# Rotary key behind the first query tile, and cross-attention values by pairs of heads, in a two-layer decoder block on one core

## The chip, the core and the metric

The kernel runs on one core of a Trainium2 chip. A core has TensorE (PE in the profile; PEld is its weight load), VectorE (DVE), ScalarE (ACT), GpSimd (POOL) and SyncE (SP), each with a queue of its own that it works through in order; DMA is issued from SyncE's queue and, in the front, from ScalarE's. The metric is device time in microseconds; less is better.

## What is computed

A block of two decoder layers over 512 tokens of width 1024, all in float32. Layer 0 mixes tokens with multi-head latent attention (MLA), layer 1 with sparse attention (DSA); each layer then attends across into 256 memory tokens with four heads of width 256, and applies a SwiGLU network (FFN). Every sub-layer ends in a residual and a layer norm. Cut to what the change touches:

```python
def mla_mixer(x, pos, w_in, q_norm, w_uq, kv_norm, w_ukv, w_o):
    h = x @ w_in                                   # 512 query, 256 key/value, 32 rotary columns
    c_q, c_kv, k_rope = h[..., :512], h[..., 512:768], h[..., 768:]
    q = (rms_norm(c_q, q_norm) @ w_uq).reshape(b, s, 16, 96)
    q = jnp.concatenate([q[..., :64], apply_rope(q[..., 64:], pos)], axis=-1)
    kv = (rms_norm(c_kv, kv_norm) @ w_ukv).reshape(b, s, 16, 128)
    k_rope = apply_rope(k_rope[:, :, None, :], pos)   # one rotary key for all heads
    ...

# cross-attention of a layer, four heads:
q = x @ w_q; k, v = mem @ w_kv[:, :1024], mem @ w_kv[:, 1024:]
out = softmax(q k^T / 16) v @ w_o
```

## The kernel before

**Products.** Every float32 operand is split into a high part (a cast on ScalarE, `split` L99) and a low part (a subtraction on VectorE, L101). `mm3` (L122 to L124) makes one product of three matmuls: high by high, high by low, low by high. `chunk` (L112) loads 512 KB of weights on SyncE's queue into a buffer `raw`, of which there are three, and splits it into `wh` and `wl`, of which there are five each. In the profile a matmul stands as out<-moving, stationary; its columns are those of the moving operand.

**Order.** The Tile framework issues the program's operations in an order of its own that follows the code's order and the operands' dependences, and sets the waits; a buffer that comes round again waits for its last reader. PSUM has two pools of four banks, "a" and "b".

**Front.** `x` transposed (four 512 KB loads, the first in two parts, SyncE) and the key/value weights `w_ckv` (304 columns, four parts c of two k each: three on ScalarE's queue, the last on SyncE, L491) are split part by part, and 8 x 12 matmuls of 304 columns make `ps2`, the 256 key/value and 48 rotary columns of four token tiles. Then the rotary key is turned: ScalarE copies each tile's rotary columns (L521, 8 copies), TensorE transposes them (L522, 4), ScalarE copies the bank to `pk` (L524). The four query tiles follow (24 matmuls of 512 columns each, weights `w_cq` in four chunks); behind each, `rms_t` normalises the key/value tile and the query tile before it: the squares on ScalarE (L530), the root on GpSimd and VectorE (L277, L279), the product on VectorE (L533), transposes on TensorE (L536), a split. Between these VectorE computes the rotary angles (`trig`, L451 to L475). The query tiles end at 51.72 us, where the value product of the heads (`mla_v`) begins.

**Cross-attention.** One stage in each layer, 251.7 to 370 us and 1011.2 to 1129.7 us. For each head hd: `scores(hd)` (24 matmuls of 256 columns and the exponentials, L426), `q_proj(hd+1)` (48 of 512), `xa_kv(hd+1)`: keys (48 of 256), values (48 of 256, weights in two chunks of the head), and `pv(hd)`: it normalises the softmax weights, turns them (8 transposes, L766), splits them, and makes 12 matmuls of 512 columns. Out-projection and residual follow.

## Time and profile before

| | us |
|---|---|
| median of 3 runs | 1540.42 (1538.08 to 1541.06) |
| profiled execution | 1538.13 |
| its span, first to last instruction | 1536.3 |
| TensorE busy | 1503.6 (98%) |
| VectorE, ScalarE, GpSimd busy | 994.9, 650.2, 303.9 |

The page gives for each engine the busy time and its share of the span; a chain of waits followed back from the last instruction; and groups of like instructions. The granted clock of TensorE is shown as a share of full speed (2.4 GHz; its other level is 1.2 GHz), 0.996 over this span. Matmuls overlap by some 0.16 us, so the pace of a run is read from start to start, not from the length of one.

### The profile page before, as it was taken

To read this page: it belongs to the slowest core of one execution; us is meant where nothing else is said; L and a number is where in the kernel's file an instruction comes from. 1 tells how busy PE (TensorE), PEld (TensorE's weight loads), DVE (VectorE), ACT (ScalarE), POOL (GpSimd) and SP (SyncE) were. 2 spreads that over 40 slices of the span, in tenths; PEclk is the share of its full clock that TensorE was granted. 3 is DMA by queue.
4 is the path that set the end of the run, shared out by engine and by line. 5 is a ranking of instruction groups with operands and counts; after the bars stand their busy time and mean duration, and the time that the engine had idled before them with its cause. 6 is when DMAs were issued, how large, how long until landed. Compare 5 with 4: busy or idle time off the path is not lost.

```text
span 1536.3 us, 20733 instructions
## 1 busy us (share of the span) xinstructions
PE 1503.6 (98%) x7902; PEld 1283.5 (84%) x7902; DVE 994.9 (65%) x1741; ACT 650.2 (42%) x1158; POOL 303.9 (20%) x299
## 2 busy tenths in 40 slices
PE   8999999999999999999999989999999999999997
PEld 7788889988898888888888787898988888888886
DVE  7787868454746665654668988675448465656545
ACT  5677753343233333332246577344332433333230
POOL 1222001000032331400024653000002322324002
PEclk9999999999999999999999999999999999999999
DMA  6233424323333232233242147333323233222221
GB/s 214 71 98 107 155 83 134 125 85 97 124 97 101 77 124 97 96 97 108 84 138 87 51 158 240 110 119 102 110 94 125 83 110 98 102 94 90 97 96 55
DMA packets 51417, 166.45 MB, mean 108 GB/s; under 512 B 5300, under 2 KB 11972, under 8 KB 49268
## 3 DMA queue, kind: packets, MB, share of 16 engines
q1 hardware_dynamic: 50740, 164.18, 32.6%
q8 instruction: 62, 1.02, 0.3%
q10 hardware_dynamic: 576, 0.93, 0.2%
q14 instruction: 39, 0.32, 0.1%
HBM read 160.86 MB, written 9.47 MB: 111 GB/s over the span
## 4 chain that ended last, share of the span: by engine, by line
PE 88%; DVE 5%; ACT 3%; DMA 2%; issue 1%; POOL 1%; SPq 0%; POOLq 0%; DVEq 0%; ACTq 0%
PE ps L122 27%; PE ps L123 27%; PE ps L124 27%; DVE t L101 2%; PE ps L336 1%; ACT wh L99 1%; ACT t L426 1%; ACT t L99 1%; DMA raw<-in_w_cq_dram 1%; PE ps L1043 1%; PE ps L644 1%; DMA t<-in_xT_dram 1%; PE ps L1060 0%; POOL wl L101 0%; DMA t<-scr 0%
## 5 line engine op out<-in xcount | busy, mean ns | idle before, releaser
L122 PE MATMUL ps<-t,wh 128*128 128x512 f32 (+1 forms) x1256 | 456.2, 364 | 3.5 <-DVE t L101 3.4
L123 PE MATMUL ps<-t,wh 128*128 128x512 f32 (+1 forms) x1256 | 455.2, 362 | 0.8 <-DVE t L101 0.8
L124 PE MATMUL ps<-t,wl 128*128 128x512 f32 (+1 forms) x1256 | 454.9, 362 | 0.0
L99 ACT CAST wh<-raw 128x1024 fp32r<-128x1024 f32 (+3 forms) x219 | 227.4, 1038 | 450.0 <-PE ps L123 167.1
L101 DVE TENSOR_TENSOR wl<-raw,wh 128x1024 fp32r<-128x1024 f32 (+2 forms) x198 | 253.2, 1280 | 218.0 <-ACT wh L99 216.3
L122 PE MATMUL ps<-wh,t 128*128 128x512 f32 (+3 forms) x838 | 305.4, 364 | 1.1 <-ACT t L426 0.9
L123 PE MATMUL ps<-wl,t 128*128 128x512 f32 (+3 forms) x838 | 303.1, 362 | 1.2 <-DVE wl L101 1.2
L124 PE MATMUL ps<-wh,t 128*128 128x512 f32 (+3 forms) x838 | 303.0, 362 | 0.2 <-DVE t L101 0.2
L122 PEld LDWEIGHTS ps<-t,wh 128*128 128x128 f32 x1256 | 237.1, 189 | 41.5 <-DVE t L101 5.5
L123 PEld LDWEIGHTS ps<-t,wh 128*128 128x128 f32 x1256 | 237.2, 189 | 37.0 <-DVE t L101 1.3
L124 PEld LDWEIGHTS ps<-t,wl 128*128 128x128 f32 x1256 | 237.1, 189 | 36.6
L122 PEld LDWEIGHTS ps<-wh,t 128*128 128x128 f32 x838 | 158.5, 189 | 25.1 <-ACT t L426 1.3
L123 PEld LDWEIGHTS ps<-wl,t 128*128 128x128 f32 x838 | 158.4, 189 | 24.6 <-DVE wl L101 1.4
L124 PEld LDWEIGHTS ps<-wh,t 128*128 128x128 f32 x838 | 158.4, 189 | 24.0 <-DVE t L101 0.4
L99 ACT CAST t<-ps 128x512 fp32r<-128x512 f32 (+2 forms) x249 | 122.9, 525 | 129.3 <-PE ps L336 86.1
L279 POOL TENSOR_TENSOR sm<-sm,mhalf 128x1 f32<-128x1 f32 x32 | 28.6, 893 | 689.0 <-DVE sm L277 689.0
L101 DVE TENSOR_TENSOR t<-ps,t 128x512 fp32r<-128x512 f32 (+2 forms) x249 | 144.1, 607 | 20.3 <-ACT t L99 19.5
L99 ACT CAST wh<-t 128x1024 fp32r<-128x1024 f32 x56 | 58.9, 1052 | 141.9 <-PE ps L123 123.6
L101 DVE TENSOR_TENSOR wl<-t,wh 128x1024 fp32r<-128x1024 f32 x56 | 71.2, 1272 | 65.2 <-ACT wh L99 63.4
L863 DVE TENSOR_TENSOR t<-ps,t 128x512 f32<-128x512 f32 x44 | 30.4, 692 | 120.1 <-PE ps L124 120.1
L101 DVE TENSOR_TENSOR t<-t,t 128x512 fp32r<-128x512 f32 (+2 forms) x113 | 84.5, 751 | 23.0 <-ACT t L99 20.7
L99 ACT CAST t<-t 128x512 fp32r<-128x512 f32 (+2 forms) x113 | 64.5, 574 | 56.2 <-POOL t L797 33.6
(178 smaller groups left out, 1654.5 us busy)
## 6 DMA issues: line engine op xcount, KB each, us to landing
raw<-in_ffn_in_dram SPq DMA_DIRECT2D x88, 512.0 KB, 3.5
...
```

The source lines that it names most:

```text
L99: nc.scalar.copy(h, src)
L101: (eng or nc.vector).tensor_tensor(l, src, h.bitcast(F32), op=ALU.subtract)
L122: nc.tensor.matmul(ps, st[0], mv[0], start=start, stop=False, skip_group_check=more)
L123: nc.tensor.matmul(ps, st[0], mv[1], start=False, stop=False, skip_group_check=more)
L124: nc.tensor.matmul(ps, st[1], mv[0], start=False, stop=stop, skip_group_check=more)
L279: nc.gpsimd.tensor_tensor(b, a, mhalf, op=ALU.pow)
L336: nc.tensor.transpose(pt[:, k], x_of(tt)[:, 512 * n + P * k:512 * n + P * k + P], ident)
L426: nc.scalar.activation(Sx, src, AF.Exp, bias=nb, scale=scale, accum_out=self.sm[:, i:i + 1])
L644: nc.tensor.transpose(pt[:, P * qt:P * qt + P], Ss[qt][:, P * kb:P * kb + P], ident)
L863: nc.vector.tensor_tensor(sg, pu, sg, op=ALU.mult)
L1043: nc.tensor.transpose(pt[:, P * i:P * i + P], Ss[i][:, P * kb:P * kb + P], ident)
```

## The change

**Front.** `w_ckv` is laid out with all eight k side by side and is loaded into three buffers (k 0 to 2, of which k 0 alone first; 3 to 5; 6 and 7), all from ScalarE's queue and at once; its high and low parts lie in three buffers each. So the `w_cq` chunks come one `raw` buffer earlier in the ring. The loads of positions and constants are issued ahead of them. The rotary key is put into a function, `rope_key`, which is called behind the normalisation of the first key/value tile, that is behind the first query tile's matmuls.

**Cross-attention.** The value weights are laid out by pairs of heads. An even head makes the values of itself and of the next one: four chunks, and 48 matmuls of 512 columns into two banks, k outermost; an odd head makes none. Normalising, turning and splitting the softmax weights is a function of its own, `turned`, and is called ahead of `xa_kv(hd+1)`.

```diff
         return res
 
     raw_x = [t8(F32) for _ in range(2)]
-    def pairs_of(tile_):
-        return tile_[:, 0:2 * NC0].rearrange("p (k m) -> p k m", k=2)
-
-    raw_w = [pairs_of(wp.tile([P, 1024], F32, tag="raw", name=nm("raw"), bufs=3)) for _ in range(3)]
+    def threes(tag, dt, bufs=5):
+        ts = [wp.tile([P, 1024], dt, tag=tag, name=nm(tag), bufs=bufs) for _ in range(3)]
+        return [t[:, 0:3 * NC0].rearrange("p (k m) -> p k m", k=3) for t in ts]
+
+    raw_w = threes("raw", F32, 3)
     xr = A["xT"].rearrange("c p (k t) -> c p k t", k=2)
-    wr = A["w_ckv"].rearrange("c p (k m) -> c p k m", k=2)
-    for i in range(2):
+    wr = A["w_ckv"].rearrange("p (k m) -> p k m", k=NK)
+    for i, ks in enumerate((slice(0, 1), slice(1, 3))):
         nc.sync.dma_start(raw_x[0][:, i], xr[0, :, i])
-        nc.scalar.dma_start(raw_w[0][:, i], wr[0, :, i])
+        nc.scalar.dma_start(raw_w[0][:, ks], wr[:, ks])
     nc.sync.dma_start(raw_x[0][:, 2:4], xr[1])
-    nc.scalar.dma_start(raw_w[1], wr[1])
-    nc.scalar.dma_start(raw_w[2], wr[2])
+    nc.scalar.dma_start(raw_w[1], wr[:, 3:6])
     nc.sync.dma_start(raw_x[1][:, 0:2], xr[2])
+    nc.scalar.dma_start(raw_w[2][:, 0:2], wr[:, 6:8])
     nc.sync.dma_start(raw_x[1][:, 2:4], xr[3])
+    posi = t2(I32)
+    nc.sync.dma_start(posi, A["positions"].broadcast_to((P, S)))
+    nc.sync.dma_start(cst, A["consts"])
     NR, NC = 73, 7
 
     def general_bias():
...
     nc.gpsimd.memset(T0[0:64], 1.0)
     nc.gpsimd.memset(T1[64:128], 1.0)
     ps2 = [bank("b") for _ in range(NT)]
+    whs, wls = threes("wh", FR), threes("wl", FR)
+    w_parts = {0: (0, 0, 1), 1: (0, 1, 3), 2: (1, 0, 3), 6: (2, 0, 2)}
     for c in range(4):
         h, l = XT[c // 2]
-        if c == 3:
-            raw_w.append(pairs_of(wp.tile([P, 1024], F32, tag="raw", name=nm("raw"), bufs=3)))
-            nc.sync.dma_start(raw_w[3], wr[3])
-        rx, rw = raw_x[c // 2], raw_w[c]
-        wh = pairs_of(wp.tile([P, 1024], FR, tag="wh", name=nm("wh")))
-        wl = pairs_of(wp.tile([P, 1024], FR, tag="wl", name=nm("wl")))
+        rx = raw_x[c // 2]
         step = 1 if c == 0 else 2
         for i in range(0, 2, step):
             k0 = 2 * (c % 2) + i
             split(h[:, k0:k0 + step], l[:, k0:k0 + step], rx[:, k0:k0 + step])
-            sw = slice(i, i + step)
-            split(wh[:, sw], wl[:, sw], rw[:, sw])
+            if 2 * c + i in w_parts:
+                t, a, b = w_parts[2 * c + i]
+                split(whs[t][:, a:b], wls[t][:, a:b], raw_w[t][:, a:b])
         for i in range(2):
             k = 2 * c + i
             xh, xl = k_of(XT, k)
             for tt in range(NT):
                 ts_ = ts_of(tt)
-                mm3(ps2[tt][:, 0:NC0], (xh[:, ts_], xl[:, ts_]), (wh[:, i], wl[:, i]), k == 0, k == NK - 1)
-    posi = t2(I32)
-    nc.sync.dma_start(posi, A["positions"].broadcast_to((P, S)))
-    nc.sync.dma_start(cst, A["consts"])
+                mm3(ps2[tt][:, 0:NC0], (xh[:, ts_], xl[:, ts_]), (whs[k // 3][:, k % 3], wls[k // 3][:, k % 3]),
+                    k == 0, k == NK - 1)
     steps = trig()
     for _ in range(2):
         next(steps)
     gq, gkv = t2(), t2()
     nc.sync.dma_start(gq, A["q_norm"].broadcast_to((P, 512)))
     nc.sync.dma_start(gkv[:, 0:256], A["kv_norm"].broadcast_to((P, 256)))
-    pkb = bank("a")
-    for tt in range(NT):
-        kr = t2(F32, (P, 2, 2, 32))
-        for a in range(2):
-            c0 = 256 + 16 * a
-            nc.scalar.copy(kr[:, a], ps2[tt][:, c0:c0 + 32].unsqueeze(1).broadcast_to((P, 2, 32)))
-        nc.tensor.transpose(pkb[:, ts_of(tt)], kr.rearrange("p a b c -> p (a b c)"), ident)
     pk = t2()
-    nc.scalar.copy(pk, pkb)
     wcq = [chunk(A["w_cq"][c], (P, 2, 512)) for c in range(4)]
+
+    def rope_key():
+
+        pkb = bank("a")
+        for tt in range(NT):
+            kr = t2(F32, (P, 2, 2, 32))
+            for a in range(2):
+                c0 = 256 + 16 * a
+                nc.scalar.copy(kr[:, a], ps2[tt][:, c0:c0 + 32].unsqueeze(1).broadcast_to((P, 2, 32)))
+            nc.tensor.transpose(pkb[:, ts_of(tt)], kr.rearrange("p a b c -> p (a b c)"), ident)
+        nc.scalar.copy(pk, pkb)
 
     def rms_t(ps, n, tt, g, dst):
         jk = t2()
...
         rms_t(ps2[tt], 256, tt, gkv[:, 0:256], ckv)
         if tt:
             rms_t(psq[tt - 1], 512, tt - 1, gq, cq)
+        if tt == 0:
+            rope_key()
         if tt < 2:
             next(steps)
     for hv in range(5):
...
                 mm3(pk[:, dt], (wh[:, k], wl[:, k]), m[k], k == 0, k == NK - 1)
         Kt = (t2(FR, (P, 2, 256)), t2(FR, (P, 2, 256)))
         split(Kt[0], Kt[1], pk)
-        ws = [chunk(A["xa_v"][i, hd, c], (P, 4, 256)) for c in range(2)]
-        pv = bank("a", (P, 2, 256))
-        for mt in range(2):
-            for k in range(NK):
+        if hd % 2:
+            return Kt, None
+        ws = [chunk(A["xa_v"][i, hd // 2, c], (P, 2, 512)) for c in range(4)]
+        pvs = [bank("a") for _ in range(2)]
+        for k in range(NK):
+            w = ws[k // 2]
+            for mt in range(2):
                 ms = slice(P * mt, P * mt + P)
-                w = ws[k // 4]
-                mm3(pv[:, mt], (m[k][0][:, ms], m[k][1][:, ms]), (w[0][:, k % 4], w[1][:, k % 4]), k == 0, k == NK - 1)
-        Vt = (t2(FR, (P, 2, 256)), t2(FR, (P, 2, 256)))
-        split(Vt[0], Vt[1], pv)
+                mm3(pvs[mt], (m[k][0][:, ms], m[k][1][:, ms]), (w[0][:, k % 2], w[1][:, k % 2]), k == 0, k == NK - 1)
+        Vt = []
+        for pv in pvs:
+            v = (t2(FR), t2(FR))
+            split(v[0], v[1], pv)
+            Vt.append(v)
         return Kt, Vt
 
     def cross(i, XT, m, kv0):
...
                 sx.exp(qt, ps[:, 0:256], 1.0 / 16.0)
             return sx
 
-        def pv(hd, sx):
+        def turned(sx):
             Ss = sx.normalise()
-            Vt = kvs[hd][1]
             PT = []
             for mb in range(2):
                 pt = bank("a")
...
                 p_ = (t2(FR), t2(FR))
                 split(p_[0], p_[1], pt)
                 PT.append(p_)
+            return PT
+
+        def pv(hd, PT):
+            Vt = kvs[hd // 2 * 2][1]
             for dt in range(2):
                 po = bank("a")
-                ds_ = slice(P * dt, P * dt + P)
+                ds_ = slice(256 * (hd % 2) + P * dt, 256 * (hd % 2) + P * dt + P)
                 for mb in range(2):
-                    mm3(po, (Vt[0][:, mb, ds_], Vt[1][:, mb, ds_]), PT[mb], mb == 0, mb == 1)
+                    mm3(po, (Vt[mb][0][:, ds_], Vt[mb][1][:, ds_]), PT[mb], mb == 0, mb == 1)
                 o = (t2(FR), t2(FR))
                 split(o[0], o[1], po)
                 OT.append(o)
...
             Ss = scores(hd, Q)
             if hd < 3:
                 Q = q_proj(hd + 1)
+            PT = turned(Ss)
+            if hd < 3:
                 kvs[hd + 1] = xa_kv(i, hd + 1, m)
-            pv(hd, Ss)
+            pv(hd, PT)
         return OT
 
     def sp_operands(e, o):
...
     f["rel_bias"] = I["rel_bias"]
     w = I["mla_w_in"][0]
     f["w_cq"] = _tm(w[:, :512], 2, 512)[0]
-    f["w_ckv"] = _tm(np.concatenate([w[:, 512:800], w[:, 768:784]], 1), 2, NC0)[0]
+    ckr = np.concatenate([w[:, 512:800], w[:, 768:784]], 1)
+    f["w_ckv"] = ckr.reshape(NK, P, NC0).transpose(1, 0, 2).reshape(P, NK * NC0)
     uq = I["mla_w_uq"][0].reshape(512, 16, 96)
     cols = []
     for h in range(16):
...
     f["dsa_o"] = _tm(I["dsa_w_o"][0], 2, 512)
     f["xa_q"] = np.stack([_fm(I["xa_w_q"][i]) for i in range(2)])
     f["xa_k"] = np.stack([_fm(I["xa_w_kv"][i][:, :1024]) for i in range(2)])
-    f["xa_v"] = np.stack([_tm(I["xa_w_kv"][i][:, 1024:], 4, 256) for i in range(2)])
+    f["xa_v"] = np.stack([_tm(I["xa_w_kv"][i][:, 1024:], 2, 512) for i in range(2)])
     f["xa_o"] = np.stack([_tm(I["xa_w_o"][i], 2, 512) for i in range(2)])
     f["ffn_in"] = np.stack([np.stack([_fm(I["ffn_w_in"][i][:, :FFN]), _fm(I["ffn_w_in"][i][:, FFN:])], 1) for i in range(2)])
     f["ffn_dg"] = np.stack([_quarters(I["ffn_w_down"][i][:FS]) for i in range(2)])
```

In the changed code the lines move by some: L521, L522, L524 become L526, L527, L528; L530, L533, L536 become L533, L536, L539; L766 becomes L775.

**TensorE, from the key/value products into the first two query tiles.** `ps_130` (before) and `ps_133` (after) are the last key/value bank, `ps_322` and `ps_298` the first query tile, `ps_367` and `ps_361` the second, `ps_279` and `ps_337` the rotary key, `ps_356` and `ps_332` key/value tile 0. Before:

```order
L124 MATMUL ps_130<-wh_227,t_10_118 128x304
L522 MATMUL ps_279<-ident,t_37_280 128x128
L522 MATMUL ps_279<-ident,t_38_284 128x128
L522 MATMUL ps_279<-ident,t_39_288 128x128
L122 MATMUL ps_322<-wh_300,t_7_115 128x512
L522 MATMUL ps_279<-ident,t_40_292 128x128
L123 MATMUL ps_322<-wl_301,t_7_115 128x512
...
L124 MATMUL ps_322<-wh_318,t_10_118 128x512
L536 MATMUL ps_356<-ident,t_59_354 128x128 x2
L122 MATMUL ps_367<-wh_300,t_7_115 128x512
```

After:

```order
L124 MATMUL ps_133<-wh_136,t_11_121 128x304
L122 MATMUL ps_298<-wh_276,t_8_118 128x512
L123 MATMUL ps_298<-wl_277,t_8_118 128x512
...
L124 MATMUL ps_298<-wh_294,t_11_121 128x512
L539 MATMUL ps_332<-ident,t_51_330 128x128 x2
L527 MATMUL ps_337<-ident,t_54_338 128x128
L527 MATMUL ps_337<-ident,t_55_342 128x128
L527 MATMUL ps_337<-ident,t_56_346 128x128
L527 MATMUL ps_337<-ident,t_57_350 128x128
L122 MATMUL ps_361<-wh_276,t_8_118 128x512
```

The four transposes of the rotary key moved from ahead of the first query tile to between the first and the second.

**VectorE, the end of the angle steps and the normalisation of query tile 0.** `t_59`, `t_66`, `t_72` (before) and `t_63`, `t_69` (after) are normalised tiles: key/value 0, key/value 1 and query 0, then key/value 1 and query 0; `t_11` and `t_12` are the split of key/value 0. Before:

```order
L101 TENSOR_TENSOR wl_542<-raw_539,wh_541 128x1024
L277 TENSOR_SCALAR sm_350<-sm_348 128x1
L472 SCALAR_TENSOR_TENSOR t_32_261<-t_33_262,t_32_261 128x512
L533 SCALAR_TENSOR_TENSOR t_59_354<-ps_127,sm_352,t_35_276 128x256
L474 TENSOR_SCALAR t_32_261<-t_32_261,cst 128x512
L277 TENSOR_SCALAR sm_395<-sm_393 128x1
L475 TENSOR_SCALAR t_32_261<-t_32_261 128x512
L533 SCALAR_TENSOR_TENSOR t_66_399<-ps_128,sm_397,t_35_276 128x256
L277 TENSOR_SCALAR sm_409<-sm_407 128x1
L533 SCALAR_TENSOR_TENSOR t_72_413<-ps_322,sm_411,t_34_275 128x512
L101 TENSOR_TENSOR t_11_119<-ps_356,t_11_119 128x2x128
```

After:

```order
L101 TENSOR_TENSOR wl_536<-raw_533,wh_535 128x1024
L476 SCALAR_TENSOR_TENSOR t_29_255<-t_30_256,t_29_255 128x512 x3
L478 TENSOR_SCALAR t_29_255<-t_29_255,cst 128x512
L479 TENSOR_SCALAR t_29_255<-t_29_255 128x512
L101 TENSOR_TENSOR t_12_122<-ps_332,t_12_122 128x2x128
L281 TENSOR_SCALAR sm_389<-sm_387 128x1
L536 SCALAR_TENSOR_TENSOR t_63_393<-ps_131,sm_391,t_32_270 128x256
L281 TENSOR_SCALAR sm_403<-sm_401 128x1
L536 SCALAR_TENSOR_TENSOR t_69_407<-ps_298,sm_405,t_31_269 128x512
```

The split of key/value tile 0 stands ahead of the normalisation of query tile 0 now, and the angle steps are all still ahead of it.

**TensorE, cross-attention of layer 0, from the query projection of head 1 to its scores.** `ps_3214` (before) and `ps_3225` (after) are that projection, `ps_3271` and `ps_3306` the keys, `ps_3348` the values of head 1 (before); `ps_3451` and `ps_3397` scores; `ps_3371` is `pv` of head 0 (after). Before:

```order
L124 MATMUL ps_3214<-t_666_2523,wl_3210 128x512
L122 MATMUL ps_3271<-t_725_2891,wh_3274 128x256
...
L124 MATMUL ps_3271<-t_732_2905,wl_3305 128x256
L122 MATMUL ps_3348<-wh_3338,t_725_2891 128x256
...
L124 MATMUL ps_3348<-wh_3344,t_733_2906 128x256
L766 MATMUL ps_3407<-ident,t_764_3157 128x128 x2
L766 MATMUL ps_3407<-ident,t_765_3158 128x128 x2
L766 MATMUL ps_3416<-ident,t_764_3157 128x128 x2
L766 MATMUL ps_3416<-ident,t_765_3158 128x128 x2
L122 MATMUL ps_3451<-t_791_3332,t_780_3263 128x256
```

After:

```order
L124 MATMUL ps_3225<-t_663_2517,wl_3221 128x512
L775 MATMUL ps_3288<-ident,t_770_3168 128x128 x2
L775 MATMUL ps_3288<-ident,t_771_3169 128x128 x2
L775 MATMUL ps_3297<-ident,t_770_3168 128x128 x2
L775 MATMUL ps_3297<-ident,t_771_3169 128x128 x2
L122 MATMUL ps_3306<-t_722_2885,wh_3309 128x256
...
L124 MATMUL ps_3306<-t_729_2899,wl_3340 128x256
L122 MATMUL ps_3371<-t_792_3293,t_754_3042 128x512
...
L122 MATMUL ps_3397<-t_804_3367,t_786_3274 128x256
```

The eight transposes moved ahead of the 48 matmuls of the keys, the values of an odd head are gone, and the 12 matmuls of `pv` stand ahead of the scores in one piece, where before they were mixed with them.

## Rows read from the trace of the kernel before

**Rows 1.** The page: busy time by engine, and the chain that ended last.
```profile
PE 1503.6 (98%) x7902; PEld 1283.5 (84%) x7902; DVE 994.9 (65%) x1741; ACT 650.2 (42%) x1158; POOL 303.9 (20%) x299
...
PE 88%; DVE 5%; ACT 3%; DMA 2%; issue 1%; POOL 1%; SPq 0%; POOLq 0%; DVEq 0%; ACTq 0%
```

**Rows 2.** Windows of the front: stretch, length, busy by engine, PEclk, DMA share, GB/s.
```profile
21.17:25.10 3.93, 0.30 (x4) 0.06 (x2) 3.02 (x6) 2.37 (x6) 0.00 (x0) 1.00 0.63 200
25.10:29.46 4.36, 4.36 (x13) 3.38 (x14) 4.22 (x7) 2.79 (x12) 0.00 (x0) 0.61 0.42 149
...
39.46:51.72 12.26, 12.26 (x63) 10.24 (x62) 7.23 (x13) 6.53 (x14) 1.64 (x3) 1.00 0.09 25
```

**Rows 3.** Timeline of TensorE, front: start, length, instruction, [idle before, releaser].
```profile
11.37 0.41 PE L123 MATMUL ps<-wl,t 128*128 128x304 f32 x1 [1.22 <-DVE wl L101]
...
21.17 0.30 PE L124 MATMUL ps<-wh,t 128*128 128x304 f32 x1
25.10 0.79 PE L522 MATMUL ps<-ident,t 128*128 128x128 f32 x3 [3.63 <-ACT t L521]
...
38.89 0.81 PE L536 MATMUL ps<-ident,t 128*128 128x128 f32 x6
39.46 0.48 PE L122 MATMUL ps<-wh,t 128*128 128x512 f32 x1
```

**Rows 4.** Timeline of ScalarE, front.
```profile
21.54 1.05 ACT L99 CAST wh<-raw 128x1024 fp32r<-128x1024 f32 x1 [2.77 <-PE ps L124]
23.77 1.04 ACT L99 CAST wh<-raw 128x1024 fp32r<-128x1024 f32 x1 [1.19 <-DMA raw<-in_w_cq_dram]
24.73 1.01 ACT L521 COPY t<-ps 128x64 f32<-128x64 f32 x8
```

**Rows 5.** SyncE's timeline of DMA issues, and the landing of the four `w_cq` loads.
```profile
7.40 0.33 SPq L491 DMA_DIRECT2D raw<-in_w_ckv_dram  x1
...
11.34 4.00 SPq L112 DMA_DIRECT2D raw<-in_w_cq_dram  x3
...
DMA to landing us min/median/max: 3.6/5.4/6.4
```

**Rows 6.** Timeline of VectorE, front, and one window (columns as in rows 2).
```profile
16.04 1.23 DVE L101 TENSOR_TENSOR wl<-raw,wh 128x1024 fp32r<-128x1024 f32 x1 [0.18 <-ACT wh L99]
...
22.62 1.23 DVE L101 TENSOR_TENSOR wl<-raw,wh 128x1024 fp32r<-128x1024 f32 x1 [0.81 <-ACT wh L99]
...
35.51 0.75 DVE L533 SCALAR_TENSOR_TENSOR t<-ps,sm,t 128x512 f32<-128x512 f32 x1 [0.66 <-POOL sm L279]
36.18 0.41 DVE L101 TENSOR_TENSOR t<-ps,t 128x256 fp32r<-128x256 f32 x1
...
14.91:36.18 21.27, 17.59 (x91) 14.89 (x90) 18.31 (x33) 10.30 (x24) 2.13 (x3) 0.92 0.56 189
```

**Rows 7.** Windows of TensorE: a query projection, then keys and values.
```profile
308.06:318.97 10.91, 10.91 (x51) 1.00 0.16 50
318.97:330.48 11.51, 11.51 (x98) 1.00 0.43 138
```

**Rows 8.** Timeline of TensorE at the second head's scores and before the out-projection.
```profile
332.42 1.06 PE L122 MATMUL ps<-t,t 128*128 128x256 f32 x3
333.32 0.28 PE L123 MATMUL ps<-t,t 128*128 128x256 f32 x1
...
366.39 0.28 PE L124 MATMUL ps<-t,t 128*128 128x256 f32 x1
367.10 0.50 PE L122 MATMUL ps<-wh,t 128*128 128x512 f32 x1 [0.43 <-ACT t L426]
```

**Rows 9.** Chunks, 300 to 345 us: cast, low part; landing of the 16 value loads.
```profile
L99 ACT CAST wh<-raw x9: 1047/1047/1058, 300.1 to 342.8; 128x1024 fp32r<-128x1024 f32 x9
L101 DVE TENSOR_TENSOR wl<-raw,wh x9: 1224/1226/1228, 301.1 to 343.9; 128x1024 fp32r<-128x1024 f32 x9
...
DMA to landing us min/median/max: 3.4/3.9/4.6
```

## The prediction

> **What bounds the kernel now.** I read the page first: TensorE is busy 98% of the span and makes up 88% of the chain that ended last [rows 1]. So only two things can shorten the kernel: less TensorE time in one of the two changed stages, or one of its few waits removed. Then I cut the front into stretches. TensorE stands still for nearly all of the 3.93 us between the last key/value product and the first key transpose, and the next 4.36 us run at a granted clock of 0.61 on the mean, mostly at the lower of the two levels, 1.2 and 2.4 GHz; later stretches show 1.00 and no gap [rows 2]. The timeline puts the two waits of the front in one place each: 1.22 us before L123 at 11.37 (VectorE has not made the low part of the weights), and 3.63 us before L522 at 25.10 (ScalarE has not made L521's copies) [rows 3]. Why ScalarE was late is in its own timeline: L521 stands at 24.73, behind four casts of `w_cq` chunks, of which the third starts at 21.54 after 2.77 us of idling [rows 4]. The profile puts that wait down to TensorE, but the buffer that the cast writes was read last by the second key/value weights, long before. SyncE issued the first chunk only at 11.34 and the third at about 15.0 (the three issues take until 15.34), and a chunk took up to 6.4 us to land [rows 5]: 21.4, just ahead of the cast. Hence the wait belongs to loading, and ScalarE's order hands it to the key. In cross-attention I read the two stages' matmuls apart by shape, then the seams between heads.
>
> **Front.** Four small steps work on one chain, so I sum them at one place, the start of the third query tile, 39.46 now [rows 3]. After that VectorE is busy 7.23 of 12.26 us [rows 2], so what is won there is kept.
> (1) Key/value weights all at once on ScalarE's queue. The fourth load is issued at 7.40 now [rows 5], because it waits for a buffer. The last TensorE product of this stage starts at 21.17 [rows 3]. Of the 1.22 us wait at 11.37 I keep about 0.2 (the low part now precedes that of the next x, but 304 KB instead of 152 KB have to land first), so the stage ends about 1.0 us sooner, at 20.3.
> (2) SyncE: positions and constants go ahead of `w_cq`, then four `w_cq` loads in a row. I put the first at about 8.5 (it was 11.34 [rows 5]), when the first key/value weights have left their buffer, and the fourth lands near 21 instead of 23.7, where the fourth cast starts [rows 4].
> (3) The key's 8 copies, 4 transposes and copy of `pk` leave the place ahead of the first tile. TensorE then goes from 20.3 straight into the tile: the 3.63 us wait goes. The transposes are done either way (4 in 0.5 to 0.8 us), and `pk` is not read before the heads.
> (4) What is late next is VectorE. From 14.91 to 36.18 it does 18.31 us of work and idles 2.96 [rows 6]; in that list are the five low parts of the weight chunks and the rotary angle steps, none of which the change removes. Its last place is L533 of the first query tile at 35.51 [rows 6], which the transposes ahead of the third tile need. These are at 38.89 now, so VectorE has 2.7 us in hand [rows 3, 6]. The change moves one 0.41 us subtraction (key/value tile 0, at 36.18 now [rows 6]) ahead of that L533. If VectorE keeps its idle, query tile 0 is ready at 36.18 + 0.41 = 36.6, six transposes take 0.57 (38.89 to 39.46 [rows 3]), and the third tile starts at 37.2. TensorE alone would be there sooner: 20.3 + 2 x 24 x 0.2275 + two sets of transposes (1.4) = 32.6; so some 4 us of waits come back, in pieces, in and between the first two tiles.
> Gain: 39.46 - 37.2 = 2.2 us. Bounds: if VectorE also loses the idle that it has for late chunks (0.18 + 0.81 of the 2.96 [rows 6]), 3.2, and with the subtraction hidden 3.6; if one chunk lands 2 us late (as 6.4 against 3.6 can be [rows 5]), 0.3. I take 2.2, as the chain of VectorE is known and the landings are not.
> The slow clock costs nothing more by this sum: nine matmuls ran at about 0.43 us instead of 0.23 [rows 2], 1.8 us, but the third tile waits for VectorE anyway. Should it recur, it is at most 0.4 us of the lasting gain.
>
> **Cross-attention, values.** Per layer 192 products of 256 columns become 96 of 512 (four heads x 48, against two pairs x 48). A run of 48 products of 512 columns, the query projection, takes 10.91 us from 308.06 to 318.97: 227.3 ns each; a run of 96 of 256 columns, keys and values, takes 11.51 us: 119.9 ns each [rows 7] (the three and two more counted there overlap a window's ends). Both layers: 384 x 119.9 ns = 46.0 us before, 192 x 227.3 ns = 43.6 us after: 2.4 us less. The bytes loaded, the casts and the splits stay the same.
> The Trainium skill, "TensorE: Matmul & The Clock Gate", section "Back-to-back issue gap", gives N / 2.4 + 2.5 ns, so 109.2 and 215.8 ns; by it the gain would be 41.9 - 41.4 = 0.5 us. The rows are 10.7 and 11.5 ns above it, so here the cost of one product is more than the columns; I go by the rows.
>
> **Cross-attention, order.** Now each head begins its products of scores right behind the transposes of the head before, whose softmax weights have yet to be split. In the second head the three products from 332.42 (one of scores, two of `pv`) take 0.90 us until 333.32, where 0.12 + 2 x 0.2275 = 0.575 would do: 0.32 us lost [rows 8]. At the fourth head the out-projection starts 0.71 us after a product worth 0.12, at 367.10 [rows 8]: it needs a bank that ScalarE's exponential frees, and the exponential stands behind casts of the same seam. In the change the eight transposes stand behind the query projection, 48 key products (5.8 us) ahead of their reader: both splits (two casts, two subtractions, under 3 us) lie under these. Behind the keys, or the values, `pv` runs at once and hides the split of the keys (2.7 us of products), and the exponential of head 3 has no product of `pv` behind it. New is that VectorE's split of the keys may stand behind a low part of a weight chunk (1.22 us [rows 9]); I allow 0.15 a layer for it, and 0.1 for what is left at the fourth head. Per layer 3 x 0.32 + 0.59 - 0.25 = 1.3 us, both 2.6. Bounds: 0 if the waits only move, 3.1 with no residue.
> Chunks: in a value pair, one is used up in 12 x 0.2275 = 2.73 us, where `raw` has three buffers. One buffer's turn is landing 3.9 (at most 4.6), cast 1.05, low part 1.23 [rows 9], with 0.2 for the issue: 6.4 to 7.1 us for three, so 2.1 to 2.4 us a chunk. It fits.
>
> **Sum.** 2.2 + 2.4 + 2.6 = 7.2 us. The profiled execution took 1538.13 us (span 1536.3 and 1.8 around it); less 7.2 it is 1530.9. It was 2.3 below the median of three runs, 1540.42; the changed kernel's median by the same step is 1533.2.
>
> **Rivals.**
> (A) The front keeps its time: landings or VectorE's steps put as much waiting into the first two tiles as L522 costs now. For it: VectorE has only 2.96 idle of 21.27 us [rows 6]. Against it: 2.7 us pass between its last step and the reader of that. Gain 0.3 to 0.9 and 5.0 from cross-attention: 1534.9.
> (B) Values cost by columns alone, as the rule of the page has it: 1.9 less gain, 1535.1. Against it: 48 and 96 products in a row that show otherwise [rows 7].
> (C) The seams' waits only move, to the split of the keys or the out-projection: 2.2 + 2.4, so 1535.8. For it: VectorE makes low parts of 1.22 us there [rows 9], behind which a split can fall.
> (D) Two of A to C together: 2 to 3.4 us of gain, 1537.0 to 1538.4; within what is no change.
> (E) Slower: four value chunks in a row run `raw` dry. Where landing exceeds 5.7 us, three turns take longer than 3 x 2.73; at 7.05 the 16 chunks lose 0.45 us each, 7.2 in all, which is the whole gain, and at 8.0 they lose 12: 1545. Against it: the longest of 16 landings is 4.6 [rows 9]; other loads of the front have taken 6.4 [rows 5].
>
> **Numbers.** Forecast 0.50, A 0.18, B 0.06, C 0.12, D 0.09, E 0.05. A difference under 0.2%, 3.1 us, cannot be told from none here. Forecast, B and most of A and C lie beyond it: faster 0.82; D and a little of A and C: same 0.13; slower 0.05. The range goes from the upper bounds (front 3.6, values 2.4, order 3.1, and 2.3 for a median as low as the profiled run is) at 1529.0 to case D at 1538.0, which leaves out E and the worst of D.
>
> **What the profile after should show.** No wait before the rotary key's transposes, now behind the first query tile, and the granted clock near 1.00 from 20 to 30 us; waits of TensorE for VectorE of 0.5 to 1.5 us in the first tile's last chunk and before the second and third tiles; the third tile at 37.2, the value stage of the heads at 49.5 instead of 51.7. In cross-attention 48 value products of 512 columns in 10.9 us, with 8 transposes right behind each query projection; no 0.71 us step before the out-projection; each of the two stages about 2.5 us shorter. I am wrong if the third tile starts after 38.9, if a value product takes more than 235 ns, or if TensorE waits for `w` chunks inside a value run.

## The result and the profile after

The changed kernel takes 1530.2 us (median of six runs, 1528.81 to 1530.61) against 1538.9 of the kernel before on the same chip: ratio 0.9941, 95% interval [0.9928, 0.9954]. That is 8.7 us less, where 7.2 were forecast. 1530.2 lies inside the range and 3.0 below the forecast of 1533.2; 1.5 of these 3.0 are the kernel before itself, whose median is 1538.9 over six runs and was 1540.4 over three. The profiled execution took 1528.81 us. Its page, against [rows 1] (busy time of TensorE, and the engines' shares of the chain that ended last):

```profile
PE 1499.2 (98%) x7710; PEld 1272.8 (83%) x7710; DVE 995.1 (65%) x1740; ACT 651.2 (43%) x1157; POOL 303.6 (20%) x299
...
PE 88%; DVE 6%; ACT 3%; POOL 1%; DMA 1%; issue 1%; POOLq 0%; SPq 0%; DVEq 0%; ACTq 0%
```

The 192 matmuls that are missing are the values of two layers, but TensorE's busy time fell by 4.4 us only, of 9.4 us in the trace: the larger part of the gain was in waits. Where it was gained is read by laying the same run of matmuls of both traces on each other and noting how much sooner it starts. At 240 us of the kernel before, behind the front, it is 3.1 us; over the first cross-attention 2.3 more; over the sparse attention 1.5 more, which nobody forecast; over the second cross-attention 2.6 more; 0.25 is given back behind that, near 1180 us (9.4 at the end).

The front of the changed kernel, timeline of TensorE, against [rows 3]:

```profile
10.49 0.41 PE L124 MATMUL ps<-wh,t 128*128 128x304 f32 x1 [0.40 <-DVE t L101]
...
20.32 0.40 PE L122 MATMUL ps<-wh,t 128*128 128x512 f32 x1
...
26.05 0.50 PE L123 MATMUL ps<-wl,t 128*128 128x512 f32 x1 [1.22 <-DVE wl L101]
...
28.46 0.44 PE L539 MATMUL ps<-ident,t 128*128 128x128 f32 x2 [0.98 <-ACT t L526]
28.74 0.76 PE L527 MATMUL ps<-ident,t 128*128 128x128 f32 x4
...
36.09 0.66 PE L539 MATMUL ps<-ident,t 128*128 128x128 f32 x4 [0.88 <-DVE t L536]
```

The first query tile starts at 20.32, right behind the key/value weights, without a wait. The 3.63 us have become three waits of 1.22, 0.98 and 0.88, each at a place that was named ahead: the first tile's last chunk, ahead of the second tile and ahead of the third, which starts at 36.50. Behind none of them does the clock fall. Windows, against [rows 2] (stretch, length, busy time of PE, PEld, DVE, ACT and POOL, granted clock, DMA share, GB/s):

```profile
20.32:25.00 4.68, 4.51 (x21) 3.38 (x19) 4.51 (x8) 2.38 (x4) 0.00 (x0) 1.00 0.82 288
25.00:29.25 4.25, 2.22 (x11) 1.51 (x12) 3.77 (x8) 1.26 (x10) 0.71 (x1) 1.00 0.36 123
29.25:32.90 3.65, 3.65 (x18) 3.02 (x18) 3.51 (x6) 2.96 (x7) 0.00 (x0) 1.00 0.45 141
36.50:48.77 12.27, 12.27 (x64) 10.23 (x62) 8.08 (x16) 5.94 (x11) 2.19 (x4) 1.00 0.09 29
```

The granted clock is 1.00 in each of these stretches, where it was 0.61 for 4.36 us; and VectorE is busy for 11.79 of the 12.58 us from 20.32 to 32.90. Its timeline there, against [rows 6]:

```profile
24.78 1.22 DVE L101 TENSOR_TENSOR wl<-raw,wh 128x1024 fp32r<-128x1024 f32 x1
...
28.76 1.22 DVE L101 TENSOR_TENSOR wl<-raw,wh 128x1024 fp32r<-128x1024 f32 x1
...
35.28 0.75 DVE L536 SCALAR_TENSOR_TENSOR t<-ps,sm,t 128x512 f32<-128x512 f32 x1 [0.66 <-POOL sm L283]
```

The first is the low part of the fourth `w_cq` chunk, for which TensorE waits 1.22 us; the second that of the first `w_v` chunk, which nobody reads before 48 us; the third normalises query tile 0, for which TensorE waits 0.88.

In cross-attention the wait view shows no wait of TensorE in the stage (two losses of 0.2 us, too short for it, are found in run 6). A value pair, and the step from head 3's scores to the out-projection, against [rows 7, 8]:

```profile
321.71 0.40 PE L122 MATMUL ps<-wh,t 128*128 128x512 f32 x1
...
332.39 0.39 PE L124 MATMUL ps<-wh,t 128*128 128x512 f32 x1
332.62 0.39 PE L122 MATMUL ps<-t,t 128*128 128x512 f32 x1
...
361.46 0.28 PE L124 MATMUL ps<-t,t 128*128 128x256 f32 x1
361.57 0.40 PE L122 MATMUL ps<-wh,t 128*128 128x512 f32 x1
```

The 48 products take 332.62 - 321.71 = 10.91 us, 227.3 ns each, to the digit what was forecast. The next is `pv` without a gap, and the out-projection follows the scores after 0.11 us instead of 0.71.

### The profile page after: what moved, and what is told of

The parts are those of the page before. It is cut to its first block, busy times and chain, and to the rows that moved or that the text cites. A ratio compares the mean times of both kernels' runs of the same rounds, so it can differ in the third digit from the quotient of the medians.

```text
span 1527.0 us, 20359 instructions
## 1 busy us (share of the span) xinstructions
PE 1499.2 (98%) x7710; PEld 1272.8 (83%) x7710; DVE 995.1 (65%) x1740; ACT 651.2 (43%) x1157; POOL 303.6 (20%) x299
## 4 chain that ended last, share of the span: by engine, by line
PE 88%; DVE 6%; ACT 3%; POOL 1%; DMA 1%; issue 1%; POOLq 0%; SPq 0%; DVEq 0%; ACTq 0%
PE ps L122 27%; PE ps L123 27%; PE ps L124 27%; DVE t L101 2%; PE ps L340 1%; ACT t L430 1%; DVE wl L101 1%; ACT wh L99 1%; DMA raw<-in_w_cq_dram 1%; POOL wl L101 1%; ACT t L99 1%; PE ps L649 1%; PE ps L1058 1%; PE ps L775 0%; PE ps L1056 0%
## 5 line engine op out<-in xcount | busy, mean ns | idle before, releaser
L99 ACT CAST wh<-raw 128x1024 fp32r<-128x1024 f32 (+2 forms) x218 | 227.2, 1042 | 447.3 <-PE ps L123 165.8
L122 PE MATMUL ps<-wh,t 128*128 128x512 f32 (+3 forms) x774 | 293.5, 379 | 0.1
L123 PE MATMUL ps<-wl,t 128*128 128x512 f32 (+3 forms) x774 | 291.2, 376 | 1.4 <-DVE wl L101 1.2
L124 PE MATMUL ps<-wh,t 128*128 128x512 f32 (+3 forms) x774 | 291.1, 376 | 0.4 <-DVE t L101 0.4
L123 PEld LDWEIGHTS ps<-wl,t 128*128 128x128 f32 x774 | 145.6, 188 | 27.3 <-DVE wl L101 2.1
L124 PEld LDWEIGHTS ps<-wh,t 128*128 128x128 f32 x774 | 145.4, 188 | 26.6 <-DVE t L101 0.7
L122 PEld LDWEIGHTS ps<-wh,t 128*128 128x128 f32 x774 | 145.6, 188 | 25.8 <-DVE t L101 0.4
```

What stands on the lines that cost most here:

```text
L99: nc.scalar.copy(h, src)
L122: nc.tensor.matmul(ps, st[0], mv[0], start=start, stop=False, skip_group_check=more)
L123: nc.tensor.matmul(ps, st[0], mv[1], start=False, stop=False, skip_group_check=more)
L124: nc.tensor.matmul(ps, st[1], mv[0], start=False, stop=stop, skip_group_check=more)
```

## The experiments

All at a glance, in us against the kernel before: start of the third query tile, and what each stage gained (front up to 240, first cross-attention, sparse attention 870 to 960, second cross-attention; + is a loss).

| kernel | third tile | front | cross 0 | sparse | cross 1 | ratio |
|---|---|---|---|---|---|---|
| changed | 36.50 | -3.1 | -2.3 | -1.5 | -2.6 | 0.9941 [0.9928, 0.9954] |
| 1 front only | 36.33 | -3.1 | 0.0 | +0.2 | -0.2 | 0.9977 [0.9968, 0.9986] |
| 2 cross only | 40.11 | +0.7 | -2.4 | -1.9 | -1.7 | 0.9961 [0.9947, 0.9975] |
| 3 key at old place | 40.22 | +0.8 | -2.3 | -2.5 | -1.8 | 0.9965 [0.9952, 0.9979] |
| 4 old loads | 36.01 | -3.5 | -2.4 | -2.3 | -2.4 | 0.9942 [0.9928, 0.9955] |
| 5 turned late | 36.65 | -2.9 | +1.1 | -1.9 | +0.9 | 0.9995 [0.9986, 1.0004] |
| 6 values by head | 36.31 | -3.1 | -1.4 | +0.1 | -1.6 | 0.9967 [0.9955, 0.9979] |
| 7 more angle steps | 37.70 | -1.8 | -2.4 | -2.3 | -1.7 | 0.9969 [0.9957, 0.9981] |
| 8 two low parts on GpSimd | 40.29 | +0.8 | -2.3 | -2.0 | -2.0 | 0.9972 [0.9961, 0.9984] |
| 9 w_v behind query tile 0 | 35.64 | -3.8 | -2.3 | -2.9 | -1.7 | 0.9948 [0.9933, 0.9962] |
| 10 key old, w_v behind | 39.29 | -0.2 | -2.3 | -2.1 | -2.5 | 0.9962 [0.9947, 0.9976] |
| 11 angle behind | 32.84 | -4.0 | -2.4 | -1.2 | -2.6 | 0.9950 [0.9936, 0.9964] |
| 12 pairs in cross 1 only | 37.21 | -2.3 | -1.4 | -2.0 | -2.6 | 0.9964 [0.9950, 0.9977] |

Where the second cross-attention shows 1.7 to 2.0 with pairs, TensorE waits 0.4 to 0.7 us for VectorE at the layer norm ahead of the stage; from behind that norm on, these kernels and the others with both stages as changed are alike to 0.1 us. The columns do not add up to a kernel's time, as such waits fall between them too: near 420 us runs 2, 4, 7, 9, 10 and 11 lose 0.3, 0.9, 1.0, 0.6, 0.8 and 0.8 us, and near 1180 run 12 loses 0.8. In each of them TensorE waits for VectorE at a layer norm, as it does not in the kernel before.

**1. The front alone** (cross-attention as before).

```diff
-        ws = [chunk(A["xa_v"][i, hd // 2, c], (P, 2, 512)) for c in range(4)]
+        ws = [chunk(A["xa_v"][i, hd, c], (P, 4, 256)) for c in range(2)]
...
-            PT = turned(Ss)
             if hd < 3:
                 kvs[hd + 1] = xa_kv(i, hd + 1, m)
-            pv(hd, PT)
+            pv(hd, Ss)
```

> The front of the change alone, cross-attention as before. Theory: the front's gain is settled by the third query tile and kept: the heads' value stage starts at 48.8 us (51.72 before, 48.77 with the whole change), and the time is 2.9 us less than before, ratio about 0.998. Rival: the front's gain is given back later (by later loads or VectorE), and the time is that of before, with the first cross-attention stage starting less than 1 us sooner than before.

As expected: the whole 3.1 us of the front are kept to the end, 0.9 more than the prediction had. The gain of the sparse attention is not there.

**2. Cross-attention alone** (front as before).

```diff
-    raw_w = threes("raw", F32, 3)
+    raw_w = [pairs_of(wp.tile([P, 1024], F32, tag="raw", name=nm("raw"), bufs=3)) for _ in range(3)]
...
-        if tt == 0:
-            rope_key()
```

> The cross-attention of the change alone, front as before. Theory: both stages are shorter by 2.4 to 2.6 us each whatever the front does, so the time is 5.0 us less than before, ratio 0.9967. Rival: part of the gain needs the other front (loads that come in another phase): under 4 us. What the sparse attention gains between the stages (1.5 us in the changed kernel's profile, which neither theory explains) should show here if the cross-attention brings it about, and in the run with the front alone if the front does.

The first stage and the sparse attention gain at least what they gain in the changed kernel; the second stage gains 1.7 of the expected 2.4 to 2.6. By the medians the kernel is 5.5 us faster, in the trace 4.9. The old front is a surprise in itself: its third and fourth `w_cq` casts start at 19.45 and 22.13, where they started at 21.54 and 23.77; TensorE waits 2.49 us ahead of the key, where it was 3.63, and again 2.42 ahead of key/value tile 0; the clock falls behind the second wait instead of the first, and the third tile starts 0.65 later than before. The same front, with other landings of its loads, waits once for 3.63 us or twice for 4.91 in all, and its third tile differs by 0.65.

**3. The key back at its old place, all else as changed.**

```diff
+    rope_key()
     wcq = [chunk(A["w_cq"][c], (P, 2, 512)) for c in range(4)]
...
-        if tt == 0:
-            rope_key()
```

> The whole change, but the rotary key is turned ahead of the first query tile again; loads as changed. Theory: VectorE's chain sets the start of the third query tile, so the key's place matters little once the loads are early: TensorE waits some 2.5 us before the key's transposes (copies behind the fourth cast, which starts at 21.5), the first tile starts at about 23.3, and the third tile at 36.2 to 36.8 us (36.50 in the changed kernel): the same time. Rival: the key's place is what gives the gain: then the third tile starts at 38 us or later, and the kernel is 1.5 to 2.9 us slower than the changed one. A clock at its lower level behind the wait would not move the third tile by the first theory.

That expectation failed by 3.4 us and more: with the new loads, but the key ahead of the first tile, nothing of the front's gain is left. Its timelines, TensorE and then VectorE:

```profile
23.22 0.79 PE L526 MATMUL ps<-ident,t 128*128 128x128 f32 x3 [2.64 <-ACT t L525]
...
32.30 0.54 PE L541 MATMUL ps<-ident,t 128*128 128x128 f32 x2 [2.73 <-DVE t L538]
32.50 0.78 PE L122 MATMUL ps<-wh,t 128*128 128x512 f32 x1
33.07 0.63 PE L123 MATMUL ps<-wl,t 128*128 128x512 f32 x1
```

```profile
29.35 1.22 DVE L101 TENSOR_TENSOR wl<-raw,wh 128x1024 fp32r<-128x1024 f32 x1
30.48 0.15 DVE L281 TENSOR_SCALAR sm<-sm 128x1 f32<-128x1 f32 x1
...
31.67 0.48 DVE L538 SCALAR_TENSOR_TENSOR t<-ps,sm,t 128x256 f32<-128x256 f32 x1 [0.45 <-POOL sm L283]
```

TensorE waits twice, and from 32.50 to 36.20 the granted clock is 0.55 (products of 0.63, 0.43 from start to start). The second wait is for the normalisation of key/value tile 0. ScalarE has its squares done by 26.1, but VectorE comes to the root at 30.48 and to the product at 31.67 (26.52 and 27.57 in the changed kernel): with the key at this place, four angle steps and the low part of `w_v` stand ahead of them in VectorE's queue. Why the framework orders them so was not found. The key's place is worth 40.22 - 36.50 = 3.7 us.

**4. The old loads, the key at its new place.**

```diff
-    raw_w = threes("raw", F32, 3)
+    raw_w = [pairs_of(wp.tile([P, 1024], F32, tag="raw", name=nm("raw"), bufs=3)) for _ in range(3)]
...
-    posi = t2(I32)
-    nc.sync.dma_start(posi, A["positions"].broadcast_to((P, S)))
-    nc.sync.dma_start(cst, A["consts"])
```

> The whole change, but the loads and buffers of the front as before; the rotary key stays behind the first query tile. Theory: TensorE goes from 21.3 us straight into the first tile, waits about 2 us for the fourth chunk's low part (at 27.4 in the kernel before), and the third tile starts at 37.2 to 37.5 us, 0.7 to 1.0 later than with the changed loads, since VectorE's chain is the same. Rival: the loads bring the gain: the third tile starts near 39.4 us as before.

No loss: the third tile starts at 36.01, 1.2 us sooner than expected. The earlier loads bring nothing that can be seen beside the 0.65 us by which landings alone move a front (run 2). With 3, the front's gain is the key's place alone.

**5. Value pairs in the old order.**

```diff
-            PT = turned(Ss)
             if hd < 3:
                 kvs[hd + 1] = xa_kv(i, hd + 1, m)
+            PT = turned(Ss)
             pv(hd, PT)
```

> The whole change, but the softmax weights are normalised, turned and split behind the next head's keys and values again; values stay in pairs. Theory: each cross-attention stage is 1.2 to 1.3 us longer than in the changed kernel (three seams of 0.3 us and the step before the out-projection), 2.5 us in all. Rival: the seams' waits were small change and the pairs gave nearly all: under 1 us in all.

Worse than expected: each stage is 0.9 to 1.1 us longer than before, 3.4 to 3.5 longer than changed, and the kernel as slow as before. Waits of TensorE in the first stage (us in total, times, longest):

```profile
PE ps L122 <- ACT t L99: 1.3, 2, 0.7
PE ps L122 <- DVE t L101: 1.0, 2, 0.5
```

An odd head makes no values, so nothing lies between its keys and the scores that read their split, and nothing hides the split of the softmax weights: pairs alone open two waits in each of heads 1 and 3, and need the new order.

**6. Values by head in the new order.**

```diff
-        ws = [chunk(A["xa_v"][i, hd // 2, c], (P, 2, 512)) for c in range(4)]
-        pvs = [bank("a") for _ in range(2)]
+        ws = [chunk(A["xa_v"][i, hd, c], (P, 4, 256)) for c in range(2)]
+        pv = bank("a", (P, 2, 256))
```

> The whole change, but the values are made head by head again, 48 products of 256 columns for each; the softmax weights are still turned ahead of the keys. Theory: 384 products of 119.9 ns in place of 192 of 227.3 ns, 2.4 us more than the changed kernel, 1.2 us in each stage. Rival (cost by columns and a small constant): 0.5 us in all.

The order alone gains 1.4 and 1.6 us; pairs on top of it 0.9 and 1.0, not 1.2. What is missing is found behind `pv`, where head 1's products of scores begin. TensorE there, in this kernel and then in the changed one, and the changed one's VectorE:

```profile
301.80 0.28 PE L122 MATMUL ps<-t,t 128*128 128x256 f32 x1
...
304.67 0.40 PE L122 MATMUL ps<-t,wh 128*128 128x512 f32 x1
```

```profile
301.09 0.40 PE L122 MATMUL ps<-t,t 128*128 128x256 f32 x2
301.43 0.39 PE L123 MATMUL ps<-t,t 128*128 128x256 f32 x1
...
304.17 0.40 PE L122 MATMUL ps<-t,wh 128*128 128x512 f32 x1
```

```profile
299.55 1.23 DVE L101 TENSOR_TENSOR wl<-raw,wh 128x1024 fp32r<-128x1024 f32 x1 [1.66 <-ACT wh L99]
300.69 1.91 DVE L101 TENSOR_TENSOR t<-ps,t 128x512 fp32r<-128x512 f32 x3
```

The 24 products take 2.87 us here and 3.08 in the changed kernel. With pairs only the 12 products of `pv` lie between the keys of head 1 or 3 and their readers, and the split of the keys (the first of the three subtractions at 300.69) stands behind the low part of a weight chunk. That is 0.2 us in head 1 and in head 3, 0.4 a stage, in every kernel with pairs and the new order. The sparse attention gains nothing here.

**7. Three more steps of 0.455 us on VectorE** (the angle plus zero, in place).

```diff
+        for _ in range(3):
+            nc.vector.tensor_scalar(ang, ang, 0.0, None, op0=ALU.add)
```

> The whole change with three more VectorE steps of 0.455 us each in the rotary angle's chain (each adds zero), ahead of the normalisation of query tile 0. Theory: VectorE's chain sets the third query tile, which starts 1.3 to 1.4 us later, at 37.8 to 37.9 us, and the heads' value stage as much later. Rival: landings or TensorE set it, and the third tile stays at 36.5 us (36.9 at most).

1.37 us more on VectorE put the third tile off by 1.2, a little less than expected: VectorE sets it.

**8. Two low parts moved to GpSimd** (the fourth `w_cq` chunk, the first `w_v` chunk).

```diff
-    wcq = [chunk(A["w_cq"][c], (P, 2, 512)) for c in range(4)]
+    wcq = [chunk(A["w_cq"][c], (P, 2, 512), nc.gpsimd if c == 3 else None) for c in range(4)]
```

> The whole change, with the low parts of the fourth query chunk and of the first head-value chunk made on GpSimd (about 2.4 us each there) in place of VectorE (1.22 us each). Theory: VectorE's chain loses 2.3 us, and TensorE itself and its wait for the fourth chunk then set the third tile, at 34.4 to 35.0 us: 1.5 to 2 us less than the changed kernel. Rival: GpSimd is late with the low part or with the roots of the normalisations queued behind it, and the third tile starts at 36.5 us or later.

This failed: the third tile starts 3.8 us later. VectorE, then GpSimd:

```profile
22.86 0.43 DVE L470 TENSOR_SCALAR t<-t 128x512 f32<-128x512 f32 x1
23.32 2.52 DVE L474 TENSOR_SCALAR t<-t 128x512 f32<-128x512 f32 x1
...
30.30 3.89 DVE L476 SCALAR_TENSOR_TENSOR t<-t,t 128x512 f32<-128x512 f32 x3
```

```profile
23.16 2.39 POOL L101 TENSOR_TENSOR wl<-raw,wh 128x1024 fp32r<-128x1024 f32 x1 [20.06 <-ACT wh L99]
...
29.84 2.35 POOL L101 TENSOR_TENSOR wl<-raw,wh 128x1024 fp32r<-128x1024 f32 x1
```

A step of VectorE that takes 0.43 takes 2.52, and ends 0.3 us after GpSimd's; three that take 2.13 take 3.89. GpSimd's 2.4 us of work took 1.8 to 2.1 from VectorE, and spared it 1.14. The Trainium skill, "SBUF — State Buffer", section "SBUF: two separate sides", says that GpSimd and VectorE, in some of its instructions, share a pair of ports, which one holds for a whole instruction while the other waits; these rows agree.

That is not all of the 3.8 us. The product of key/value tile 0 comes at 29.90 instead of 27.57, and TensorE:

```profile
30.80 0.69 PE L539 MATMUL ps<-ident,t 128*128 128x128 f32 x2 [3.77 <-ACT t L526]
...
39.72 0.82 PE L539 MATMUL ps<-ident,t 128*128 128x128 f32 x6
```

Behind the wait of 3.77 us the granted clock is 0.50, from 30.80 to 36.41, and nine products take 0.43 each and the first 0.57, about 2 us more in all. Query tile 0 is normalised at 37.44, but the third tile follows the second without a wait: here TensorE sets it.

**9. The low part of `w_v` held behind query tile 0.** `norm` keeps the normalising instructions.

```diff
-                wts["v"] = chunk(A["w_v"][h // 8], (P, 2, 512))
+                wts["v"] = chunk(A["w_v"][h // 8], (P, 2, 512), after=(None, norm["q", 0] if h == 0 else None))
```

> The changed kernel, but the low part of w_v's first chunk (one subtraction of 1.1 us on VectorE) is held back until VectorE has normalised query tile 0. Theory (VectorE's chain of angle steps, low parts and normalisations sets the third query tile): the normalisation comes about 1.1 us earlier, the wait of 0.88 us in front of the turning of query tile 0 goes, the third tile starts at 35.5 to 35.7 us instead of 36.50, mla_v at 47.8 to 48.0, and the time falls by 0.8 to 1.0 us against the changed kernel. Rival (something other than VectorE is due at the same time, ScalarE's copies or the low part of the fourth chunk of w_cq): the wait stays at 0.6 or more and the third tile starts at 36.2 or later.

As expected in the trace: the wait is gone, and the third tile starts 0.86 sooner. TensorE:

```profile
34.75 0.39 PE L124 MATMUL ps<-wh,t 128*128 128x512 f32 x1
34.98 0.91 PE L539 MATMUL ps<-ident,t 128*128 128x128 f32 x6
35.64 0.48 PE L122 MATMUL ps<-wh,t 128*128 128x512 f32 x1
```

The trace ends 0.8 us sooner than that of the changed kernel (10.2 against 9.4), but the ratios of the two can't be told apart.

**10. The key at its old place, and `w_v` held behind key/value tile 0** (the edit of 3, and that of 9 with `norm["kv", 0]`).

```diff
+    rope_key()
...
+                wts["v"] = chunk(A["w_v"][h // 8], (P, 2, 512), after=(None, norm["kv", 0] if h == 0 else None))
```

> The kernel with the key back ahead of the first query tile, and the low part of w_v's first chunk held back until VectorE has normalised key tile 0. It shortens the second of the two waits of that kernel (2.73 us at the turning of key tile 0) to about 1.6 us and leaves the first (2.64 us) as it was. Theory A (the length of the wait is what costs, and the lower clock comes behind the long wait): with about 1.6 us the clock stays at 1.00 from 30 to 37 us, and the third query tile starts at 37.2 to 37.6 us. Theory B (the lower clock belongs to the place of the key and not to the length of the second wait): the clock still falls to about 0.6 behind it, and the third tile starts at 38.6 to 39.1 us. A third: the wait does not shrink, since another step of VectorE or ScalarE takes its place, and the third tile stays at 40 us.

The third case, nearly: the angle's steps (26.05 to 29.67 on VectorE) take the place of the low part, and the second wait shrinks by 0.26 us only. Timeline and window of TensorE:

```profile
31.35 0.44 PE L541 MATMUL ps<-ident,t 128*128 128x128 f32 x2 [2.47 <-DVE t L538]
```

```profile
31.54:35.64 4.10, 4.10 (x14) 3.19 (x14) 2.99 (x8) 3.09 (x6) 2.01 (x2) 0.61 0.36 122
```

The clock falls as before, and the third tile starts at 39.29. So A and B are not told apart.

**11. The angle's steps in the order in which TensorE needs VectorE** (with the edit of 9).

```diff
-    for _ in range(2):
-        next(steps)
+    next(steps)
...
-        if tt < 2:
-            next(steps)
+        if tt < 3:
+            with behind(norm["q", tt - 1] if tt else norm["kv", 0]):
+                next(steps)
```

> The changed kernel with VectorE's work put in the order in which TensorE needs it: the low part of w_v's first chunk behind the normalisation of query tile 0, the second round of the angle's steps behind the normalisation of key tile 0, the third behind that of query tile 0, the last behind that of query tile 1. Theory (VectorE's chain sets the front, its angle steps are not due before the first rotary step): no wait at the fourth chunk of w_cq (its low part is done near 23.8 us), the second query tile starts near 26.7 us, the third near 32.8, mla_v near 45.1, and the time is about 3.5 us less than the changed kernel's, near 1526.7 us. Rival (something else is late next, or the angle comes due at the first rotary step and puts it back there): the third tile starts at 35 us or later, or mla_v gives the gain back, and the time is within 1 us of the changed kernel's.

In the front each number comes as worked out: no wait, second tile 26.71, third 32.84, `mla_v` 45.10. Then it is mostly given back; TensorE, then VectorE:

```profile
45.10 0.36 PE L122 MATMUL ps<-wh,t 128*128 128x256 f32 x1
...
48.21 0.39 PE L122 MATMUL ps<-wh,t 128*128 128x256 f32 x1 [1.45 <-DVE t L101]
...
55.15 0.50 PE L123 MATMUL ps<-t,wh 128*128 128x512 f32 x1 [1.29 <-DVE t L101]
```

```profile
44.28 3.48 DVE L101 TENSOR_TENSOR wl<-raw,wh 128x1024 fp32r<-128x1024 f32 x3
```

Three low parts of the heads' weights stand ahead of key/value tile 3, as that block of VectorE's work has come due. Of 3.7 us on the changed kernel 1.0 is left at 110 us, and near 420, where the FFN's first chunks land 4.4 us after their issue (median of four; 3.8 in the changed kernel), VectorE comes late to the layer norm behind one of their low parts, and TensorE waits 0.75 for it, another 0.8 goes. The time can't be told from that of the changed kernel: the rival held, in that the gain was given back.

**12. Pairs in the second cross-attention only.** Its edit takes the lines of 6 where `i == 0`.

```diff
-            Vt = kvs[hd // 2 * 2][1]
+            Vt = kvs[hd if i == 0 else hd // 2 * 2][1]
```

> The changed kernel with the values of the first cross-attention computed head by head again (in the new order), those of the second by pairs. It asks where the unforecast 1.5 us of the sparse attention, which lies between the two, comes from: all seven profiles with both stages by pairs had it, all three with both by heads had not. Theory A (it hangs on what the first cross-attention leaves behind, its buffers or its instructions): the gain between 870 and 960 us goes, the shift there is within 0.3 us of zero, and the read of the scratch rows lands 6.5 us or more after its issue. Theory B (it does not hang on the first stage, but on the program's layout as a whole or on chance): the gain of 1.5 to 2.5 us stays and the read lands in 5.1 to 5.6 us. For both: the first cross stage gains 1.3 to 1.6 us against the kernel before instead of 2.3, the second 2.4 to 2.6, the front 2.9 to 3.1.

Theory B: the sparse attention gains 2.0 us although the first stage works head by head; the stages gain 1.4 and 2.6 as expected. The front gains 2.3 only, against 2.9 to 3.1: the third `w_cq` chunk is cast at 19.20 instead of 18.85, and VectorE's chain is late by 0.35 from there. TensorE:

```profile
26.41 0.50 PE L123 MATMUL ps<-wl,t 128*128 128x512 f32 x1 [1.54 <-DVE wl L101]
...
28.82 0.44 PE L539 MATMUL ps<-ident,t 128*128 128x128 f32 x2 [0.96 <-ACT t L526]
...
29.75 0.78 PE L122 MATMUL ps<-wh,t 128*128 128x512 f32 x1
...
36.63 0.82 PE L539 MATMUL ps<-ident,t 128*128 128x128 f32 x6
```

Behind these two waits the granted clock falls, as it does not in the changed kernel: it is 0.64 from 29.75 to 33.60, five products take 0.43 each and the first 0.58, about 1.3 us more in all. So TensorE ends the second tile 1.8 later than in the changed kernel, with query tile 0 ready by then, and itself sets the third tile, at 37.21, 0.7 later.

What the gain of the sparse attention is made of is seen in the kernel before (TensorE's wait in the sparse attention, and the reads of the scratch rows, issued from 918 to 936 us: count, KB each, median us to landing):

```profile
PE ps L1026 <- DVE sm L420: 1.3, 1, 1.3
```

```profile
t<-scr SPq DMA_DIRECT2D x3, 1024.0 KB, 6.8
```

and in this one:

```profile
t<-scr SPq DMA_DIRECT2D x4, 1024.0 KB, 5.7
```

There VectorE waits for a read that lands late, and TensorE for VectorE. With any stage by pairs the read landed sooner and the wait was gone, in all eleven profiles; with none it was there, in all three. Between 930 and 950 us the eleven gain 1.8 to 2.2 us, runs 1 and 6 nothing; the rest of the table's column, up to 1 us either way, comes from ahead of that. What in the program makes the read slow was not found.

## Why the prediction was right, point by point

**Front, forecast 2.2, measured 3.0 to 3.1.** Step 1 holds: first tile at 20.32, forecast 20.3. Step 2 holds as a fact (first `w_cq` chunk issued at 7.77, the fourth cast at 21.49) and is worth nothing (run 4). Here the reading ahead of the sum failed: "Hence the wait belongs to loading, and ScalarE's order hands it to the key". With the old loads nothing is lost, with the key at its old place all of it is. Landings do move the wait (3.63 or 2.49 us with the same front, run 2), but with the shorter one the third tile starts 0.65 later, not sooner. In this the front's forecast was lucky: the change moved the key together with the loads. The old place costs twice: TensorE waits for the copies, and again for the normalisation of key/value tile 0, which VectorE reaches late. Step 4 holds: VectorE is late next and sets the third tile (7, 9), where the clock does not fall. It was mis-sized by 0.7: query tile 0 was ready at 36.6 by the sum, and its normalisation came at 35.28 for 0.75 us, so at 36.0. The sum had kept VectorE's work and idle as they were and added 0.41. From 14.91 to 35.95 it was busy for 18.18 of 21.04 us, against 18.31 of 21.27 with the moved subtraction left out [rows 6]: 18.31 + 0.41 - 18.18 = 0.54 of its work and 0.10 of its idle no longer lie in the stretch.

"The slow clock costs nothing more by this sum" was not tested by the change, whose front keeps the full clock. Where the clock fell at the transposes of key/value tile 0 (2, 3, 8, 10, 12), TensorE and not VectorE set the third tile: in 3 and 10 some eight products at 0.43 instead of 0.23, about 1.6 us.

**Values, forecast 2.4, measured 1.9.** The pace is right to the digit, 227.3 ns (rival B is out). Runs 6 and 12 leave 0.9 to 1.0 a stage for pairs, not 1.2. The 0.4 a stage that the scores of heads 1 and 3 lose (run 6) more than cover the difference; what gives the rest back was not found.

**Order, forecast 2.6, measured 3.0.** 1.4 and 1.6. With the values by head, the 0.25 a stage that were allowed for what might be left were hardly needed; that is near the upper bound, 3.1. With pairs, the split of the keys does fall behind a low part, as the prediction feared: it allowed 0.15 a stage and 0.4 are lost, which stand under the values above.

**Sparse attention, forecast nothing, measured 1.5.** Not in the sum, and luck: nobody knew of it. The four make 3.1 + 1.9 + 3.0 + 1.5 = 9.5, against 9.4 at the end of the trace and 8.7 in the medians. The total of 7.2 came as near as it did because the values, 0.5 too high, offset some of the rest, all too low.

**Rivals.** A is out (run 1), and D with it and B. C is what happens without the new order (run 5), and with it to 0.4 a stage. E is out: with four chunks in a row no wait of TensorE for a weight chunk is seen.

**Open.** Why the clock falls behind some waits: it fell behind 3.63 (before), 2.42 (run 2), 2.73 (3), 2.47 (10) and 3.77 us (8), and behind the two of 1.54 and 0.96 us in run 12; it did not behind 2.64 (3), 2.49 (2) and 1.90 us (10), each of these the first wait behind the key/value products, nor behind the two of 1.22 to 1.42 and 0.98 us in the changed kernel and in 5, 7 and 9. The length of a wait alone does not decide it. Open too is why VectorE's order changes with the key's place (3).
